# The first MLP product of a hybrid decoder layer, for three of its four groups, as seven quarter-block products on normalised tokens

## The chip, the cores and the metric

One core of one Trainium2 chip runs the whole layer as one program. The metric is the time of one execution in microseconds on the device, as the median of several runs. All data are float32. A product is made of "fp32r" operands, a float32 format of TensorE: every operand is split into a high part and a low remainder, and a product is the sum of three matmuls (low by high, high by low, high by high).

## The reference

The layer has a retention branch, a latent attention branch, an output projection, an MLP and a gated per-layer embedding. Only the MLP and what stands around it is touched:

```python
h2 = rms_norm(x, norm_mlp)                       # x: 512 tokens x 1024
x = x + jnp.square(jax.nn.relu(h2 @ w_up)) @ w_down   # w_up 1024 x 4096, w_down 4096 x 1024
gate = jax.nn.sigmoid(rms_norm(x, norm_ple) @ w_ple_gate)
x = x + gate * (p_l @ w_ple)
```

`rms_norm` divides each token by the root of its mean square and multiplies each of the 1024 channels by a gain.

## The kernel before

Activations lie transposed: 128 channels on the partitions, 512 tokens along the row, so the 1024 channels are 8 tiles. The 4096 features of the MLP are worked in `GROUPS` = 4 groups of 1024.

**The first product ("up").** For each group, `up` makes 8 tiles of 128 features, each from 8 channel tiles by `mm3`, that is 24 matmuls with 512 moving columns. Its right side are the tokens `x2g`, which carry the gain but not the token's factor; `up_out` multiplies by that factor (`bcx2`, one row broadcast to all partitions), takes the positive part on VectorE and squares on ScalarE. The result of a group is two tiles `F[gg, 0]` and `F[gg, 1]`, each 4 feature tiles by 512 tokens.

**The second product ("dn").** It is already done by seven quarter-block products, a scheme like Strassen's: the group's operands (features by tokens, and features by output channels) are cut into 2 by 2 blocks, and seven products of sums of blocks give what eight products of blocks would. The products carry the numbers 1, 7, 2, 6, 5, 4, 3. `combine` makes the token side of each (differences of quarters of `F`, then the split into high and low, tiles `ch` and `cl`); `down` does the 24 matmuls of a product in two halves c = 0, 1 (keys `("sw", ("dn", gg), p, c)`), each with its own weight chunk of 512 KB; `down_out` adds the finished product into the sum `d`.

**The weight side of the seven products** is made by the DMAs. `prepare` loads a chunk with SP's queue (`nc.sync`), and where the product needs a sum of two blocks, POOL's queue adds the second block onto the same buffer in memory order (`more`, `accum_op=ALU.add`, L222). Products 1, 7, 2, 5 and 3 take one plain load for each half; products 7, 5, 6 and 4 take one adding transfer for each half, and 7, 6 and 4 work on one and the same buffer one after the other: the next block is added when the last product's split has read the buffer. So a set of seven products has 10 plain loads and 8 adding transfers of 512 KB. Buffers for plain loads (`wraw`) are 6, those for the 7-6-4 sums (`draw`) 4.

**The split of a chunk** (`load_chunk`): ScalarE copies it to the high part (L260), VectorE subtracts for the low part (L264). High and low parts have `NW` = 3 buffers each, so the split of a key can start when the third key before it has been multiplied.

**The order.** `step` records a list; `run_steps` emits it, with loads up to `PREP` keys ahead; the framework then schedules each engine, except that matmuls keep the order of the list. Within a group pair the order is `seq = [1, "u", 7, "u", 6, 2, "u", 5, 4, "u", 3]`: products of "dn" of group gg, with a quarter (`up_pair`) of "up" of group gg + 1 at each "u". Each engine works its queue strictly in order, SP's and POOL's DMA queues too. After the last group come `ple`, `turn` (transposes `d` back and adds the residual), `ple_gate` and `ple_out`.

Of the kernel before, what the change touches and what calls it, by code (L numbers as in the profile page):

```python
# [31 lines left out]
F32R = mybir.dt.float32r  # L32
# [34 lines left out]
def _rng(a, n):  # L67
    return np.arange(a, a + n)


def chunk_specs():

    spec = {}

    def add(key, name, rows, cols):
        spec[key] = (len(rows) // P * len(cols), lambda w: _tiles(w[name], rows, cols))

    half = ROPE // 2
# [68 lines left out]
def trunk_layer(ctx: ExitStack, tc: tile.TileContext, xT, pT, pos, gains, const, decay, wstream, outT):  # L147
# [68 lines left out]
    def prepare(key):  # L216

        if key[0] == "sw":
            _, blk, p, c = key

            def more(raw, kb, fb):
                nc.gpsimd.dma_start(raw, chunk(("w", blk, kb, fb, c)), accum_op=ALU.add)  # L222

            if p in (6, 4):
                return more(dw[blk, "t", c], *((0, 0) if p == 6 else (1, 0)))
            kb, fb = {1: (0, 0), 7: (0, 1), 2: (1, 0), 5: (0, 1), 3: (1, 1)}[p]
            nm = f"{blk[0]}{blk[1]}{p}{c}"
# [12 lines left out]
        nm = "_".join(str(x) for x in key)  # L240
        raw = wpool.tile([P, width], F32, tag="wraw", name="wr_" + nm, padded_shape=[P, 1024], bufs=NRAW)
        tc.keep_in_program_order(nc.sync.dma_start(raw, chunk(key))) if key[0] == "a1" else nc.sync.dma_start(raw, chunk(key))
        dw[key] = raw

    def load_chunk(key):

        sign = 1.0
        if key[0] == "sw":
            _, blk, p, c = key
            raw = dw[blk, "t" if p in (7, 6, 4) else p, c]  # L250
            nm = f"{blk[0]}{blk[1]}{p}{c}"
            if p in (1, 4) and blk[0] != "dn":
                sign = -1.0
        else:
            raw = dw[key]
            nm = "_".join(str(x) for x in key)
# [719 lines left out]
    def up_out(gg, pair):  # L976
# [5 lines left out]
            STT(u[:, i], ps[:, i], 0.0, V["bcx2"], op0=ALU.max, op1=ALU.mult)  # L982
        ACT(u, u, AF.Square)

    def xsplit(gg, p, src, scale=None):
# [56 lines left out]
    def ple_in():  # L1042
        t = A("praw", (2, S), "cs", 2)
        nc.sync.dma_start(t, pT)
        V["pph"] = A("pph", (2, S), "pph", 1, F32R)
        V["ppl"] = A("ppl", (2, S), "ppl", 1, F32R)
        split(t, None, hi=V["pph"], lo=V["ppl"])

    pw, x3 = [], []
# [9 lines left out]
        pw.extend([t[:, 0], t[:, 1]])  # L1059

    def reload_x2():
        for j in range(2):
            t = A(f"x3{j}", (4, S), "x3" if j else "f", 1 if j else 4)
            nc.sync.dma_start(t, x2d[:, 4 * j:4 * j + 4])
            x3.append(t)

    def turn(n):

        ps, t = PP(f"tr{n}"), x3[n // 2][:, n % 2 * 2:n % 2 * 2 + 2]
# [28 lines left out]

    def ple_out(n):
        N = S // len(pg_ps[n])  # L1100
        z = A(f"zg{n}", (S,), "z", 2)
        for c, ps in enumerate(pg_ps[n]):
            cs = slice(c * N, c * N + N)
            TT(z[:, cs], ps, V["bcx3"][:, cs], op=ALU.mult)
            ACT(z[:, cs], z[:, cs], AF.Sigmoid)
            TT(z[:, cs], z[:, cs], pw[n][:, cs], op=ALU.mult)
            TT(z[:, cs], z[:, cs], x3[n // 4][:, n % 4, cs], op=ALU.add)
            nc.sync.dma_start(outT[n * P:n * P + P, cs], z[:, cs])


# [164 lines left out]
        step(("o", n), out_proj, n)  # L1275
    step(None, open_tail)

    def up_pair(gg, pair):
        for n in (2 * pair, 2 * pair + 1):
            step(("up", gg, n), up, gg, n)  # L1280
            if (gg, n) == (0, 0):
                step(None, token_stats, "x2", "sq2")
            elif (gg, n) == (0, 1):
                step(None, token_factor, "x2")
        step(None, up_out, gg, pair)

    for pair in range(4):
        up_pair(0, pair)

    seq = [1, "u", 7, "u", 6, 2, "u", 5, 4, "u", 3]  # L1290
    order = [p for p in seq if p != "u"]
    step(None, combine, 0, 1)
    for gg in range(GROUPS):
        u = 0

        for p in seq if gg + 1 < GROUPS else [1, 7, 2, "u", 6, "u", 5, 4, 3]:
            if p == "u":
                if gg + 1 < GROUPS:
                    up_pair(gg + 1, u)
                else:  # L1300
                    if u == 0:
                        step(None, ple_in)
                    step(("ple", u // 2), ple, u)
                u += 1
                continue
            if gg == GROUPS - 1:
                order = [1, 7, 2, 6, 5, 4, 3]
            i = order.index(p)
            if p != 3:
                step(None, combine, gg, order[i + 1])  # L1310
            elif gg + 1 < GROUPS:
                step(None, combine, gg + 1, 1)
            if gg == GROUPS - 1 and p == 6:
                step(None, reload_x2)
            for c in range(2):
                step(("sw", ("dn", gg), p, c), down, gg, p, c)
                if gg == GROUPS - 1 and p == 3 and c == 0:
# [65 lines left out]
```

## Time and profile before

| what | value |
|---|---|
| median of 3 runs | 1105.74 us (1105.18 to 1105.89) |
| the profiled execution: its time | 1106.31 us |
| the profiled execution: its span | 1104.5 us |
| TensorE busy | 1093.7 us, 99% of the span |
| VectorE busy | 711.1 us, 64% |
| ScalarE busy | 541.1 us, 49% |
| plain transfers (SP's queue) | 129.66 MB, 34.6% of the 16 DMA engines' span |
| POOL's transfers | 47.46 MB, 21.6% |

The span runs from the first to the last instruction; the execution's own time is 1.8 us longer. "Busy" is the time in which at least one instruction of the engine is under way; TensorE's matmuls overlap each other, so a matmul's listed duration is longer than its share of the time, and the pace is read from the distance of two starts. The DMA share is the sum of the packets' times over 16 engines, and can pass 1 a little where packets overlap.

### The profile page before, as it was taken

Reading aid. Unit: us, or ns where it says so; the run is one execution under the profiler, and the core shown is the slowest. Engines: PE = TensorE matmul, PEld = TensorE weight load, DVE = VectorE, ACT = ScalarE, POOL = GpSimd, SP = SyncE. Lnnn points to the kernel's source line nnn. Section 1 sums busy time; section 2 is a strip of 40 time slices with the busy share of each in tenths; the row PEclk is TensorE's granted clock in tenths of the full one; section 3 lists DMA queues with packets and bytes.
Section 4 is the critical chain, followed back from the end, with each engine's and each line's share of the span. In section 5 each row is a group of like instructions: output and inputs, shape, how many; then the busy total and the mean of one; then the engine's idle time right before and its main releaser. Section 6 shows DMA issues by size and latency. Waiting matters only on the chain.

```text
span 1104.5 us, 13845 instructions
## 1 busy us (share of the span) xinstructions
PE 1093.7 (99%) x5137; PEld 910.8 (82%) x5137; DVE 711.1 (64%) x1135; ACT 541.1 (49%) x785; POOL 89.9 (8%) x121
## 2 busy tenths in 40 slices
PE   9999999999999999999999999999999999999998
PEld 6778888888888888888888887888888888888887
DVE  7697677556774654656465577555556656658685
ACT  7647556444456545355654634434544444445542
POOL 0000000001111001121100100010100100101000
PEclk9999999999999999999999999999999999999999
DMA  7242231366789635488864944693765765738511
GB/s 258 72 120 87 72 106 54 128 208 205 207 194 246 195 143 171 116 202 205 209 207 115 268 142 158 193 276 103 181 172 150 184 182 136 190 116 219 147 54 58
DMA packets 59860, 178.02 MB, mean 161 GB/s; under 512 B 7376, under 2 KB 8784, under 8 KB 59536
## 3 DMA queue, kind: packets, MB, share of 16 engines
q1 hardware_dynamic: 45168, 129.66, 34.6%
q0 software_dynamic: 14480, 47.46, 21.6%
q8 instruction: 40, 0.66, 0.2%
q14 instruction: 28, 0.23, 0.1%
q10 hardware_dynamic: 144, 0.03, 0.0%
HBM read 157.97 MB, written 17.04 MB: 158 GB/s over the span
## 4 chain that ended last, share of the span: by engine, by line
PE 92%; DVE 4%; ACT 1%; issue 1%; DMA 1%; SPq 0%; DVEq 0%; ACTq 0%
PE up L167 16%; PE dn L167 14%; PE rv L167 7%; PE rg L167 7%; PE br L167 6%; PE pg L167 4%; PE gr L167 4%; PE rk L167 4%; PE bm L167 4%; PE rq L167 4%; PE wo L167 4%; PE gm L167 3%; PE ro L167 2%; PE sc L167 2%; PE pcq L167 1%; PE rs L167 1%
## 5 line engine op out<-in xcount | busy, mean ns | idle before, releaser
L167 PE MATMUL dn<-wh_dn,cl 128*128 128x512 f32 x224 | 87.2, 389 | 0.0
L167 PE MATMUL dn<-wh_dn,ch 128*128 128x512 f32 x224 | 87.1, 389 | 0.0
L167 PE MATMUL dn<-wl_dn,ch 128*128 128x512 f32 x224 | 87.1, 389 | 0.0
L260 ACT ACTIVATE wh_dn<-wr_dn 128x1024 fp32r<-128x1024 f32 x32 | 34.0, 1062 | 75.4 <-PE up L167 54.3
L260 ACT ACTIVATE wh_up<-wr_up 128x1024 fp32r<-128x1024 f32 x32 | 33.9, 1061 | 57.7 <-PE up L167 29.3
L264 DVE TENSOR_TENSOR wl_dn<-wr_dn,wh_dn 128x1024 fp32r<-128x1024 f32 x32 | 39.0, 1220 | 27.5 <-ACT wh_dn L260 27.5
L264 DVE TENSOR_TENSOR wl_up<-wr_up,wh_up 128x1024 fp32r<-128x1024 f32 x32 | 39.1, 1222 | 18.6 <-ACT wh_up L260 18.6
L167 PEld LDWEIGHTS dn<-wh_dn,cl 128*128 128x128 f32 x224 | 42.0, 188 | 8.8
L167 PEld LDWEIGHTS dn<-wh_dn,ch 128*128 128x128 f32 x224 | 42.0, 188 | 8.7
L982 DVE SCALAR_TENSOR_TENSOR f<-up,bcx 128x512 f32<-128x512 f32 x32 | 20.6, 685 | 44.4 <-PE up L167 44.4
L167 PEld LDWEIGHTS dn<-wl_dn,ch 128*128 128x128 f32 x224 | 42.0, 188 | 8.6
L260 ACT ACTIVATE wh_dn<-dr_dn 128x1024 fp32r<-128x1024 f32 x24 | 25.4, 1060 | 42.5 <-PE up L167 29.4
L260 ACT ACTIVATE wh_rg<-wr_rg 128x1024 fp32r<-128x1024 f32 x28 | 29.6, 1059 | 31.1 <-PE rg L167 12.1
L260 ACT ACTIVATE wh_rv<-wr_rv 128x1024 fp32r<-128x1024 f32 x28 | 29.6, 1058 | 30.6 <-PE rv L167 11.0
L222 POOL DMA_DIRECT2D dr_dn<-wstream x24 | 21.1, 890 | 289.4 <-DMA dr_dn<-wstream 165.0
L264 DVE TENSOR_TENSOR wl_dn<-dr_dn,wh_dn 128x1024 fp32r<-128x1024 f32 x24 | 29.3, 1222 | 22.4 <-ACT wh_dn L260 22.4
L264 DVE TENSOR_TENSOR wl_rg<-wr_rg,wh_rg 128x1024 fp32r<-128x1024 f32 x20 | 24.5, 1226 | 23.6 <-ACT wh_rg L260 23.6
L264 DVE TENSOR_TENSOR wl_rv<-wr_rv,wh_rv 128x1024 fp32r<-128x1024 f32 x20 | 24.4, 1223 | 18.0 <-ACT wh_rv L260 18.0
L1040 DVE TENSOR_TENSOR d<-d,dn 128x1024 f32<-128x1024 f32 x24 | 29.2, 1219 | 6.5 <-PE dn L167 6.5
L264 DVE TENSOR_TENSOR wl_br<-wr_br,wh_br 128x1024 fp32r<-128x1024 f32 x16 | 19.5, 1221 | 19.3 <-ACT wh_br L260 19.3
L260 ACT ACTIVATE wh_br<-wr_br 128x1024 fp32r<-128x1024 f32 x16 | 16.9, 1059 | 21.0 <-issue 12.8
L871 ACT ACTIVATE rt<-br 128x512 f32<-128x512 f32 x24 | 13.9, 593 | 25.9 <-PE br L167 25.9
(1819 smaller groups left out, 3440.7 us busy)
## 6 DMA issues: line engine op xcount, KB each, us to landing
wr_up<-wstream SPq DMA_DIRECT2D x32, 512.0 KB, 4.1
wr_dn<-wstream SPq DMA_DIRECT2D x32, 512.0 KB, 3.4
dr_dn<-wstream POOLq DMA_DIRECT2D x24, 512.0 KB, 7.6
wr_rv<-wstream SPq DMA_DIRECT2D x20, 512.0 KB, 4.4
wr_rg<-wstream SPq DMA_DIRECT2D x20, 512.0 KB, 5.3
wr_rv<-wstream POOLq DMA_DIRECT2D x16, 512.0 KB, 6.3
wr_rg<-wstream POOLq DMA_DIRECT2D x16, 512.0 KB, 7.4
wr_br<-wstream SPq DMA_DIRECT2D x16, 512.0 KB, 3.9
```

The source lines that it names most:

```text
L167: return tc.keep_in_program_order(nc.tensor.matmul(*a, **k))
L222: nc.gpsimd.dma_start(raw, chunk(("w", blk, kb, fb, c)), accum_op=ALU.add)
L260: i = ACT(hi, raw, AF.Copy, scale=sign)
L264: TT(lo, raw, hi.bitcast(F32), op=ALU.subtract)
L871: ACT(t, ps, AF.Copy)
L982: STT(u[:, i], ps[:, i], 0.0, V["bcx2"], op0=ALU.max, op1=ALU.mult)
L1040: TT(to, to, dps[p], op=ALU.add if sign > 0 else ALU.subtract)
```

## The change

The first 1024 features (group 0) keep the plain product. For groups 1, 2 and 3 "up" becomes seven quarter-block products too.

- **Tokens.** `up_norm` loads the residual `x2` back from device memory (two transfers of 1 MB) and multiplies it by gain and token factor, so that the products need no factor afterwards. `up_operand` makes the token side of each of the seven products once, as high and low tiles of 512 columns each, and keeps them for all three groups: in the 16 tiles that held `x2g`, in five new buffers "xs", and in the two tiles that held `bcx2` and the sum of squares.
- **Matmuls.** `up_seven` does a half product as 4 feature tiles by 2 channel tiles by 3 matmuls, each with 256 moving columns: 24 a key, 48 a product, 336 a group where there were 192 with 512 columns.
- **Results.** Products 1, 7 and 6 are copied out by ScalarE; 2, 5 and 4 are added or subtracted and then rectified and squared by VectorE (two instructions on 1024 columns); 3 is rectified by VectorE and squared by ScalarE. `up_out` with its 8 products by the factor is left for group 0 alone.
- **Weights.** Each of the three groups has 10 plain loads and 8 adding transfers of 512 KB for "up" where it had 8 plain loads; the buffer of product 7 comes from `draw`, now shared by "dn" and "up".
- **Order.** `seq` has products of both: 1, 7, 2, 6 of "dn", then "u1", 5, "u7", 4, "u6", 3, and "u2", "u5", "u4", "u3" without a "dn" between them.
- **Small moves** for the room: `reload_x2` brings the residual in three transfers, `pph`, `ppl` use "xs", and `ple_out` writes to the halves of a two-tile buffer.

```diff
     for gg in range(GROUPS):
-        for n in range(8):
+        for n in range(0 if gg else 8):
             add(("up", gg, n), "w_up", full, _rng((8 * gg + n) * P, P))
...
+                    if gg:
+                        add(("w", ("up", gg), kb, fb, c), "w_up", _rng(kb * S + c * 2 * P, 2 * P), _rng(gg * D + fb * S, S))
...
-            if p == 7 and blk[0] == "dn":
+            if p == 7 and blk[0] in ("dn", "up"):
                 raw = tail_pool["w"].tile([P, 1024], F32, tag="draw", name="dr_" + nm, bufs=NDRAW)
...
+    def up_norm(j):
+
+        t = F["x", j] = A(f"x2n{j}", (4, S), "f", 4)
+        nc.sync.dma_start(t, x2d[:, 4 * j:4 * j + 4])
+        for k in range(4):
+            STT(t[:, k], t[:, k], g(G_MLP + 4 * j + k), V["bcx2"], op0=ALU.mult, op1=ALU.mult)
+
+    def up_operand(p):
+
+        f1, f2 = F["x", 0], F["x", 1]
+        a11, a21, a12, a22 = f1[:, :, 0:256], f1[:, :, 256:512], f2[:, :, 0:256], f2[:, :, 256:512]
+        if p == 7:
+            TT(a11, a21, a11, op=ALU.subtract)
+        elif p == 6:
+            TT(a11, a22, a11, op=ALU.subtract)
+            TT(a21, a21, a22, op=ALU.subtract)
+        elif p == 3:
+            TT(a11, a12, a11, op=ALU.subtract)
+        src = {1: a11, 7: a11, 6: a11, 3: a11, 2: a12, 5: a21, 4: a22}[p]
...
+        for c, (hi, lo) in enumerate(zip(*pairs)):
+            split(src[:, 2 * c:2 * c + 2], None, scale, hi=hi, lo=lo)
+            XU[p].extend((hi[:, k], lo[:, k]) for k in range(2))
+
+    def up_seven(w, gg, p, c):
+
+        ch = CHAIN[p]
+        if c == 0 and p in (1, 7, 2):
+            ups[ch] = PP(f"us{gg}{p}")
+        ps = ups[ch].rearrange("p a (b c) -> p (a b) c", b=2)
+        for o in range(4):
+            for k in range(2):
+                mm3(ps[:, o], cut(w, k * S + o * P), XU[p][2 * c + k], p in (1, 7, 2) and c + k == 0 and o % 2 == 0,
+                    c + k == 2, skip_group_check=True)
+        if c == 0:
+            return
...
+        if p in (1, 7, 6):
+            ACT(t, ps, AF.Copy, scale=1.0 if p == 7 else -1.0)
+        elif p == 3:
+            TS(t, ps, 0.0, None, op0=ALU.max)
+            ACT(t, t, AF.Square)
+        else:
+            TT(t, t, ps, op=ALU.subtract if p == 4 else ALU.add)
+            STT(t, t, 0.0, t, op0=ALU.max, op1=ALU.mult)
...
-    seq = [1, "u", 7, "u", 6, 2, "u", 5, 4, "u", 3]
+    order = [1, 7, 2, 6, 5, 4, 3]
+    seq = [1, 7, 2, 6, "u1", 5, "u7", 4, "u6", 3, "u2", "u5", "u4", "u3"]
```

Three places show how the instructions move.

TensorE, where "up" of group 1 begins behind a product of "dn" of group 0. Before (`up` is the result in PSUM, `x2g` the tokens, `wh` and `wl` the weights' parts):

```order
L167 MATMUL dn_6907<-wh_dn_6901,ch_6891 128x512
L167 MATMUL up_6949<-x2g0h,wl_up_0_6921 128x512
L167 MATMUL up_6949<-x2g0l,wh_up_0_6920 128x512
L167 MATMUL up_6949<-x2g0h,wh_up_0_6920 128x512
L167 MATMUL up_6949<-x2g1h,wl_up_0_6921 128x512
```

and now (`us` is the result, `xu1` the tokens of product 1):

```order
L169 MATMUL dn_6943<-wh_dn_7099,ch_7035 128x512
L169 MATMUL us_7144<-xu1h,wl_up_7118 128x256
L169 MATMUL us_7144<-xu1l,wh_up_7117 128x256
L169 MATMUL us_7144<-xu1h,wh_up_7117 128x256
L169 MATMUL us_7144<-xu1h,wl_up_7118 128x256
```

The matmuls of "up" have half the columns; those of "dn" stay.

VectorE in the first products of "dn" of group 0, from the split of product 7's first chunk to that of product 6's second (`wl`: a weight chunk's low part; `s` and `cl`: token sums and their low parts for "dn"; `f`: the rectified features; `d`: the sum). Before:

```order
L264 TENSOR_TENSOR wl_dn_6975<-dr_dn_6924,wh_dn_6974 128x1024
L306 TENSOR_TENSOR cl_7114<-f_6823,ch_7113 128x1024
L264 TENSOR_TENSOR wl_dn_7014<-dr_dn_6946,wh_dn_7013 128x1024
L982 SCALAR_TENSOR_TENSOR f_7004<-up_6949,bcx_6692 128x512 x2
L264 TENSOR_TENSOR wl_up_2_7033<-wr_up_2_6978,wh_up_2_7032 128x1024
L264 TENSOR_TENSOR wl_up_3_7051<-wr_up_3_7017,wh_up_3_7050 128x1024
L264 TENSOR_TENSOR wl_dn_7081<-dr_dn_6924,wh_dn_7080 128x1024
L306 TENSOR_TENSOR cl_7157<-s_0_7154,ch_7156 128x1024
L264 TENSOR_TENSOR wl_dn_7118<-dr_dn_6946,wh_dn_7117 128x1024
```

and now the middle of that stretch, from product 7's second chunk on (`xu`: the new token operands):

```order
L266 TENSOR_TENSOR wl_dn_6998<-dr_dn_6940,wh_dn_6997 128x1024
L313 SCALAR_TENSOR_TENSOR xu4l_7041<-x2n_6768,xu4h_7039 128x512
L1006 TENSOR_TENSOR x2n_6698<-x2n_6768,x2n_6698 128x4x256
L266 TENSOR_TENSOR wl_dn_7017<-wr_dn_6960,wh_dn_7016 128x1024
L308 TENSOR_TENSOR cl_7036<-s_6921,ch_7035 128x1024
L313 SCALAR_TENSOR_TENSOR xu4l_7042<-x2n_6768,xu4h_7040 128x512
L266 TENSOR_TENSOR wl_dn_7057<-wr_dn_7001,wh_dn_7056 128x1024
L308 TENSOR_TENSOR xu3l_7050<-x2n_6698,xu3h_7048 128x512
L1076 TENSOR_TENSOR s_0_7093<-f_6694,f_6835 128x1024
L308 TENSOR_TENSOR xu3l_7051<-x2n_6698,xu3h_7049 128x512
L266 TENSOR_TENSOR wl_dn_7075<-dr_dn_6880,wh_dn_7074 128x1024
```

The weight splits of product 2 and 6 now stand behind token operands of later products, in one queue.

POOL's adding transfers, from the pair that makes product 7's sum for the second group of "dn" to the pair that makes product 6's in the same buffers. Before:

```order
L222 DMA dr_dn_7480<-wstream 128x1024
L222 DMA dr_dn_7500<-wstream 128x1024
L222 DMA dr_dn_6924<-wstream 128x1024
L222 DMA dr_dn_6946<-wstream 128x1024
L222 DMA wr_dn_7183<-wstream 128x1024
L222 DMA wr_dn_7203<-wstream 128x1024
L222 DMA dr_dn_6924<-wstream 128x1024
L222 DMA dr_dn_6946<-wstream 128x1024
L222 DMA dr_dn_8034<-wstream 128x1024
L222 DMA dr_dn_8054<-wstream 128x1024
L222 DMA dr_dn_7480<-wstream 128x1024
L222 DMA dr_dn_7500<-wstream 128x1024
```

and now:

```order
L224 DMA dr_dn_7668<-wstream 128x1024
L224 DMA dr_dn_7707<-wstream 128x1024
L224 DMA dr_up_7173<-wstream 128x1024
L224 DMA dr_up_7211<-wstream 128x1024
L224 DMA dr_up_7905<-wstream 128x1024
L224 DMA dr_up_7943<-wstream 128x1024
L224 DMA wr_dn_7853<-wstream 128x1024
L224 DMA wr_dn_7873<-wstream 128x1024
L224 DMA dr_dn_7668<-wstream 128x1024
L224 DMA dr_dn_7707<-wstream 128x1024
```

Before, the sum for product 7 stood a whole group ahead: behind it come products 6, 5 and 4 of the group before. Now it stands behind those, and between it and product 6 come the last pair of "up" of this group, the first of "up" of the next, and the pair of product 5.

More of the change, by code (lines that the diff above doesn't have):

```diff
@@ L251, in load_chunk @@
             nm = f"{blk[0]}{blk[1]}{p}{c}"
-            if p in (1, 4) and blk[0] != "dn":
+            if p in (1, 4) and blk[0] not in ("dn", "up"):
                 sign = -1.0
@@ L1061, in reload_x2 @@
     def reload_x2():
-        for j in range(2):
-            t = A(f"x3{j}", (4, S), "x3" if j else "f", 1 if j else 4)
-            nc.sync.dma_start(t, x2d[:, 4 * j:4 * j + 4])
+        t = A("x30", (4, S), "f", 4)
+        nc.sync.dma_start(t, x2d[:, 0:4])
+        x3.extend((t[:, 0:2], t[:, 2:4]))
+        for j in range(2, 4):
+            t = A(f"x3{j}", (2, S), "xs", 5)
+            nc.sync.dma_start(t, x2d[:, 2 * j:2 * j + 2])
             x3.append(t)
     def turn(n):
-        ps, t = PP(f"tr{n}"), x3[n // 2][:, n % 2 * 2:n % 2 * 2 + 2]
+        ps, t = PP(f"tr{n}"), x3[n]
         for i in range(2):
@@ L1100, in ple_out @@
         N = S // len(pg_ps[n])
-        z = A(f"zg{n}", (S,), "z", 2)
+        if n % 2 == 0:
+            V["zg"] = A(f"zg{n}", (2, S), "cs", 2)
+        z = V["zg"][:, n % 2]
         for c, ps in enumerate(pg_ps[n]):
@@ L1276, in trunk_layer @@
     step(None, open_tail)
[L1278 to L1288, printed above, removed]
-    seq = [1, "u", 7, "u", 6, 2, "u", 5, 4, "u", 3]
-    order = [p for p in seq if p != "u"]
+    for n in range(8):
+        step(("up", 0, n), up, 0, n)
+        if n == 0:
+            step(None, token_stats, "x2", "sq2")
+        elif n == 1:
+            step(None, token_factor, "x2")
+        if n % 2:
+            step(None, up_out, 0, n // 2)
+        if n in (1, 3):
+            step(None, up_norm, n // 2)
+        elif n in (5, 7):
+            step(None, up_operand, 1 if n == 5 else 7)
@@ L1292, in trunk_layer @@
+    order = [1, 7, 2, 6, 5, 4, 3]
+    seq = [1, 7, 2, 6, "u1", 5, "u7", 4, "u6", 3, "u2", "u5", "u4", "u3"]
     step(None, combine, 0, 1)
     for gg in range(GROUPS):
[L1294 to L1304, printed above, removed]
-                continue
-            if gg == GROUPS - 1:
-                order = [1, 7, 2, 6, 5, 4, 3]
-            i = order.index(p)
-            if p != 3:
[L1310 to L1313, printed above, removed]
+        last, quarter = gg + 1 == GROUPS, 0
+        for p in [1, 7, 2, "e", 6, "e", 5, 4, 3] if last else seq:
+            if p == "e":
+                if quarter == 0:
+                    step(None, ple_in)
+                step(("ple", 0), ple, quarter)
+                quarter += 1
+                continue
+            if type(p) is str:
+                for c in range(2):
+                    step(("sw", ("up", gg + 1), int(p[1]), c), up_seven, gg + 1, int(p[1]), c)
+                if p == "u5":
+                    step(None, combine, gg + 1, 1)
+                continue
+            if p != 3:
+                step(None, combine, gg, order[order.index(p) + 1])
+            if gg == 0 and p in (1, 7, 2):
+                for m in {1: (6,), 7: (2, 5), 2: (4, 3)}[p]:
+                    step(None, up_operand, m)
+            if last and p == 6:
@@ L1316, in trunk_layer @@
                 step(("sw", ("dn", gg), p, c), down, gg, p, c)
-                if gg == GROUPS - 1 and p == 3 and c == 0:
+                if last and p == 3 and c == 0:
                     step(None, turn, 0)
```

23 lines of the change are left out of this document (20 added, 3 removed).

## Prediction

> **What bounds the kernel now.** First I read the page's first lines: how long, and who is busy.
>
> ```profile
> span 1104.5 us, 13845 instructions
> PE 1093.7 (99%) x5137; PEld 910.8 (82%) x5137; DVE 711.1 (64%) x1135; ACT 541.1 (49%) x785; POOL 89.9 (8%) x121
> ```
>
> TensorE never rests for long, but that is an average; what counts is the stage that changes. So next the chain of waits in order of time (start, length, what), in the MLP:
>
> ```profile
> 724.49 32.67 PE up L167 x144
> 757.16 5.44 PE dn L167 x24
> 762.60 10.88 PE up L167 x48
> ...
> 833.32 10.88 PE dn L167 x48
> ...
> 914.92 10.88 PE dn L167 x48
> ...
> 985.64 10.88 PE up L167 x48
> 996.52 21.76 PE dn L167 x96
> ```
>
> Each piece begins where the one before ends: TensorE alone sets the end. The piece at 833.32 is product 3 of one group and product 1 of the next, as is that at 914.92: a group takes 914.92 - 833.32 = 81.60 us. 48 matmuls take 10.88 us, so 512 columns cost 0.2267 us each; 192 of them for "up" are 43.52 us, 168 for "dn" 38.08 us, together 81.6. Nothing else is in it, so a saved matmul is saved time, for as long as what feeds TensorE keeps up.
>
> **The matmuls.** Removed: 3 x 192 of 512 columns. Added: 3 x 336 of 256, with the same 128 x 128 stationary side. Half the columns is not half the time if something is fixed, so I looked for matmuls of that shape; the value products have it (timeline, start and listed duration):
>
> ```profile
> 181.73 0.28 PE L167 MATMUL pv<-wl_v,ckv0h 128*128 128x256 f32 x1
> ...
> 184.35 0.28 PE L167 MATMUL pv<-wh_v,ckv1h 128*128 128x256 f32 x1
> ```
>
> 22 steps between these two starts: 2.62 / 22 = 0.1191 us, 53% of 0.2267. The page "TensorE: Matmul & The Clock Gate" of the Trainium skill (Back-to-back issue gap) gives 262 cycles for 256 columns and 518 for 512, which is 51%; by it, estimated at 2.4 GHz, a group would gain 4.8 us. No row here is that fast, and I stay with the rows: 336 x 0.1191 = 40.02 us in place of 43.52, **3.5 us a group, 10.5 us in all**. Both ends of this are close (every run of such matmuls in the trace keeps this pace), so the term is firm; the question is what it costs elsewhere.
>
> **VectorE.** Every weight chunk of 512 KB needs one subtraction, and a key is now 24 x 0.1191 = 2.86 us where it was 5.44. Steps of a packed stretch:
>
> ```profile
> 920.78 1.21 DVE L1040 TENSOR_TENSOR d<-d,dn 128x1024 f32<-128x1024 f32 x1
> 921.92 1.22 DVE L264 TENSOR_TENSOR wl_up<-wr_up,wh_up 128x1024 fp32r<-128x1024 f32 x1
> 923.05 1.22 DVE L306 TENSOR_TENSOR cl<-s,ch 128x1024 fp32r<-128x1024 f32 x1
> ```
>
> An instruction on 1024 columns takes a slot of 1.14 us. A later group needs 28 weight splits, 7 sums into d, 7 low parts and 4 differences for "dn", and 7 for the results of "up": 53 x 1.14 = 60.4 us of now 78.1 (77%). Before it was 49.76 of 81, the first row here:
>
> ```profile
> 757.00:838.00 81.00, 81.00 (x359) 67.08 (x358) 49.76 (x47) 37.95 (x37) 6.93 (x8) 1.00 0.60 161
> 838.00:920.00 82.00, 82.00 (x364) 67.89 (x363) 51.36 (x49) 35.06 (x34) 6.89 (x8) 1.00 0.62 169
> 297.00:319.00 22.00, 22.00 (x99) 18.22 (x98) 17.35 (x25) 15.55 (x22) 4.30 (x5) 1.00 0.95 201
> ```
>
> (Columns: window, its length, busy time of PE, weight load, DVE, ACT, POOL, clock, DMA share, GB/s.) In the retention's seven products, the third row, VectorE is busy 17.35 of 22 us (79%) and TensorE does not stop, so the mean is bearable. The worst place is the passage to a new group: "up" ends in three products with two or more instructions each, and products 1, 7, 2 follow with a sum, a difference and a low part each. Counted along the order from the end of "u2", the split of product 6's first chunk is about the 27th in line and done some 1 us before it is needed. I price it at 0, at most 1 us a group.
>
> Group 0 is worse. There the token operands are made: 8 factor products and 14 low parts on 512 columns and 4 differences on 1024, all on VectorE. Row for 512 columns: x2 in 1.29 us, so 0.6 us a slot.
>
> ```profile
> 757.20 1.29 DVE L982 SCALAR_TENSOR_TENSOR f<-up,bcx 128x512 f32<-128x512 f32 x2 [3.12 <-PE up L167]
> 758.40 1.21 DVE L264 TENSOR_TENSOR wl_up<-wr_up,wh_up 128x1024 fp32r<-128x1024 f32 x1
> ```
>
> 22 x 0.6 + 4 x 1.14 = 17.8 us. Those before 757 are covered by plain "up" keys of 5.44 us. From the last features of group 0 (757.2) the queue holds, up to the split of product 6's second chunk: 2 x 0.6 features, 6 splits, 6 pieces for "dn" (one of them the sum of product 2), 1 token difference, and 5 token low parts of 0.6: 13 x 1.14 + 7 x 0.6 = 19.0 us. That ends at 776.2, or up to 1 us later where TensorE's last reads of the old tokens hold up those in front; needed at 757.16 + 16.32 + 2.72 = 776.2. So 0 to 1 us late, if the reloaded residual is there in time. It comes from here:
>
> ```profile
> x<-x2d SPq DMA_DIRECT2D x2, 1024.0 KB, 11.0
> dr_dn<-wstream POOLq DMA_DIRECT2D x24, 512.0 KB, 7.6
> ```
>
> Two transfers of 1 MB are issued where before one was, at 721.7; at 11 us for one they land near 733 and 740. VectorE waits at the second's first use with the rest of its queue behind it, the splits of the last "up" keys and all above. With 740 the whole list shifts by some 3 us. Ends: 0 and 4 us; I take **2 us** for group 0, the middle, since the second transfer is the one that shares the engines with four adding ones.
>
> **ScalarE** gets 28 x 1.06 for weights, 7 for "dn" and 4 for "up" a group, 41 us of 78, in its queue right ahead of VectorE; hidden, at no cost.
>
> **DMA.** A group had 18 plain loads and 8 adding transfers; it gets 20 and 16. Prices from windows with one kind alone:
>
> ```profile
> 373.00:389.40 16.40, 16.40 (x74) 13.59 (x73) 12.26 (x14) 9.05 (x11) 0.00 (x0) 1.00 0.55 192
> 848.00:858.00 10.00, 10.00 (x46) 8.29 (x45) 4.47 (x5) 3.31 (x4) 1.71 (x2) 1.00 0.63 107
> 864.00:870.00 6.00, 6.00 (x28) 4.99 (x27) 1.28 (x2) 1.06 (x1) 1.80 (x3) 1.00 1.02 193
> ```
>
> First row, plain: 0.55 x 16.4 = 9.0 us for 192 x 16.4 = 3149 KB, six chunks of 524 KB, 1.5 us each. Second, two adding ones: 6.3 us, 3.1 each; third, adding ones back to back: 524 / 193 = 2.7 us each. With 2.9 the old group is 18 x 1.5 + 8 x 2.9 = 50.2 us, 0.61 of 82: the row at 838 has 0.62. The new group is 20 x 1.5 + 16 x 2.9 = **76.4 us of 78.1**; with 2.7, 73.2. This is the tight resource. "DMA: Bandwidth & Descriptors" of the Trainium skill (Issuing engines are not separate DMA queues) says that transfers of all issuers run on the same 16 engines; that speaks against this change, and the third row agrees, where POOL's alone fill them. If POOL's queue had engines of its own, its 16 x 2.9 = 46 us would leave plenty of room.
>
> How close to full have they run without holding TensorE? 0.95 over 22 us above, and longer:
>
> ```profile
> 329.00:369.00 40.00, 40.00 (x178) 33.14 (x177) 21.73 (x33) 24.81 (x38) 8.18 (x11) 1.00 0.93 235
> 462.00:542.00 80.00, 80.00 (x362) 66.65 (x361) 39.96 (x52) 40.89 (x60) 16.70 (x20) 1.00 0.91 212
> ```
>
> PE is busy throughout both. Now 0.94 to 0.98 for three groups. The place where it decides is product 6 of "dn": its block is added to product 7's buffer after that one's split, 16 us after the group's start, and POOL must first have served the first pair of "up" and the pair of product 5, which themselves wait for loads and buffers. From 15 us before the group's start to 15 after, 8 loads (product 7's buffer and product 1 of "up", products 5 and 3 of "dn") and 6 adding ones (7 of "up", 5 and 6 of "dn") fall due: 12 + 17 = 29 us of 30. So product 6 is just in time or late by a few us. Ends: 0, and 4.5 a group (below); I take 1.5 us for the two passages inside the stage, **3 us**. In the last group `ple` stands ahead of product 6, and little else is fetched: 0.
>
> **The rest.** `ple_out`, the split residual reload and the shared "xs" buffers move no work and stand where the DMA has room: 0.
>
> **Sum**, against the profiled execution's 1106.31: -10.5 + 2 + 3 = -5.5, 1100.8. The median of the runs is 0.57 below that execution, so 1105.74 - 5.5 = **1100.2**.
>
> **Rivals.**
>
> *A. Everything is covered.* The retention's stage at 0.95 speaks for it; that was 22 us, not 234, speaks against. Then only group 0 may cost up to 1: 1105.74 - 10.5 = 1095.2 to 1096.
>
> *B. The adding transfers become the bound.* If the engines give no more over a group than the 0.91 to 0.93 of the long windows, a group takes 76.4 / 0.92 = 83 us against 81.6: 3 x 1.4 + 2 for group 0 = +6.2, 1112. It decides from the point where the share needed per group (0.98 by 2.9 us, 0.94 by 2.7) passes what the queues sustain. For it: POOL's queue is in order and waits for splits, so gaps can't be made up; against: when TensorE slows, the demand falls, and 1.02 is on record for short.
>
> *C. The gain is eaten to nothing:* product 6 late by 2.5 us at each passage and group 0 by 4, about -1.5: 1104, within what the measurement tells from no change (0.2%, 2.2 us).
>
> *D. The half-wide matmuls take half the time*, 0.1133: then 336 take 38.1 us, 5.4 less a group, and with the same stalls it is 1105.74 - 16.3 + 5 = 1094.4. Against it: the rows keep 0.119 over all 22 steps. The skill's page named above points this way, without reaching it.
>
> **How the numbers follow.** The forecast (TensorE's gain less 3 to 7 us of stalls, 1098.2 to 1102.2) has 0.48; A 0.18; D 0.03; C 0.15; B 0.16. Faster by over 0.2% (below 1103.5): forecast, A and D, 0.69; within 0.2%: C, 0.15; slower: B, 0.16. Range: from A's end, 1095.5, up to 1107.0, which takes in C and the start of B and leaves out the worse half of B.
>
> **What would show it.** Right: 48 matmuls of "us" in 5.7 us on the chain; short pieces of DVE or ACT in it near product 6 of "dn" and near 757 to 777; DMA share about 0.95 in the MLP. A: no such pieces. B: POOL or DMA pieces on the chain at every group, TensorE idle over 4 us a group, adding transfers landing in well over 7.6 us. Wrong altogether: matmuls of 256 columns at another pace than 0.119, or a wait for PSUM or for "us" results by TensorE, which I price at 0: between a product and the next that writes onto the same sum at least one other passes, 5.4 us or more, against 1.2 us to read it out.

## The result, and the profile after

| | before | changed kernel |
|---|---|---|
| median | 1105.82 us (4 runs) | 1119.79 us (4 runs, 1119.01 to 1120.34) |
| ratio | | 1.0126, 95% interval 1.0113 to 1.0139 |
| the profiled execution: its time | 1106.31 us | 1120.34 us |

The kernel became slower by 14 us, where 5.5 us less were forecast. The first lines of the page after, and its list of DMA issues (transfer, queue, count, size, median time from issue to landing):

```profile
span 1118.6 us, 14885 instructions
PE 1091.0 (98%) x5569; PEld 924.0 (83%) x5569; DVE 757.5 (68%) x1176; ACT 565.9 (51%) x817; POOL 111.3 (10%) x145
...
dr_dn<-wstream POOLq DMA_DIRECT2D x24, 512.0 KB, 7.0
...
dr_up<-wstream POOLq DMA_DIRECT2D x18, 512.0 KB, 9.6
```

TensorE is still "98% busy" and its busy time has hardly changed (1093.7 before): a matmul that runs slowly, and the overlap of the last one with a wait, both count as busy. The share doesn't show what happened. The chain of waits in order of time does (start, length, what):

```profile
823.16 17.29 PE us L169 x144
...
846.38 4.35 DMA wr_dn<-wstream
...
851.29 0.49 POOL wr_dn L224
...
851.84 0.55 POOL dr_dn L224
852.38 13.93 DMA dr_dn<-wstream
...
866.42 1.07 ACT wh_dn L262
...
867.51 1.24 DVE wl_dn L266
...
868.79 2.79 PE dn L169 x11
871.58 5.75 PE us L169 x48
...
884.42 0.56 POOL dr_up L224
884.98 11.62 DMA dr_up<-wstream
...
899.08 3.13 PE us L169 x24
...
907.68 17.29 PE us L169 x144
```

Before, pieces of TensorE followed on one another here. Now, twice in a group, the chain leaves TensorE: for an adding transfer of "dn" (13.93 us) and one of "up" (11.62 us), each followed by its split. The first piece is one product's second half coming late: the plain load of product 5 lands at 850.73 (846.38 + 4.35), then POOL issues product 5's second add, then product 6's second add, which lands 13.93 us later.

What TensorE waited for from 712 us to the end (in all, times, longest), and the windows of two stretches in the MLP (columns as in the prediction):

```profile
PE dn L169 <- DVE wl_dn L266: 9.4, 9, 2.8
PE us L169 <- DVE wl_up L266: 4.1, 5, 1.2
PE dn L169 <- ACT wh_dn L262: 2.9, 2, 1.5
```

```profile
757.00:850.00 93.00, 86.08 (x523) 75.77 (x522) 69.61 (x67) 53.15 (x58) 14.12 (x17) 0.98 0.83 213
850.00:940.00 90.00, 85.35 (x530) 76.21 (x529) 67.35 (x58) 42.74 (x42) 17.27 (x20) 1.00 0.90 218
```

TensorE waits, and yet the DMA engines are less busy (0.83, 0.90) than the 0.91 to 0.95 that the prediction found beside a TensorE that never stopped. VectorE, at 69.61 us of 93 and 67.35 of 90, isn't full either. The waits named "DVE" are waits for a split, and the split waits for a transfer.

**Where the 14 us are.** The first matmul of each "dn" product 1 marks a group's start. The timeline has these at 756.99, 846.03, 930.55 and 1015.31 us:

```profile
756.99 0.39 PE L169 MATMUL dn<-wh_dn,cl 128*128 128x512 f32 x1
...
846.03 0.40 PE L169 MATMUL dn<-wh_dn,cl 128*128 128x512 f32 x1
...
930.55 0.40 PE L169 MATMUL dn<-wh_dn,cl 128*128 128x512 f32 x1
...
1015.31 0.40 PE L169 MATMUL dn<-wh_dn,cl 128*128 128x512 f32 x1
```

So the passages take 89.04, 84.52 and 84.76 us, where one took 81.60 before. A passage without any wait takes 78.48 us (experiment E1 below). The excess is 10.6, 6.0 and 6.3, together 22.9 us; TensorE's own gain is 3 x 3.12 = 9.4. The difference is 13.5 of the 14.03 us between the two profiled executions. As for the rest, the last group with all that follows it takes 103.3 us instead of 102.5, and group 0 starts 0.2 us sooner. By place, from the starts of the products in the same timeline:

| passage | "dn" products 1, 7, 2, 6 | product 6 of "up", and the one before it | all |
|---|---|---|---|
| group 0 to 1 | 10.1 us | 0.5 us | 10.6 |
| group 1 to 2 | 3.6 us | 2.4 us | 6.0 |
| group 2 to 3 | 3.8 us | 2.5 us | 6.3 |

### The profile page after: what moved, and what is told of

Its sections match the earlier page's. It is cut to its first block, busy times and chain, and to the rows that moved or that the text cites. A ratio compares the mean times of both kernels' runs of the same rounds, so it can differ in the third digit from the quotient of the medians.

```text
span 1118.6 us, 14885 instructions
## 1 busy us (share of the span) xinstructions
PE 1091.0 (98%) x5569; PEld 924.0 (83%) x5569; DVE 757.5 (68%) x1176; ACT 565.9 (51%) x817; POOL 111.3 (10%) x145
## 3 DMA queue, kind: packets, MB, share of 16 engines
q0 software_dynamic: 17936, 60.04, 27.6%
## 5 line engine op out<-in xcount | busy, mean ns | idle before, releaser
L169 PEld LDWEIGHTS dn<-wl_dn,ch 128*128 128x128 f32 x224 | 42.5, 190 | 21.5 <-DVE wl_dn L266 13.5
L266 DVE TENSOR_TENSOR wl_up<-dr_up,wh_up 128x1024 fp32r<-128x1024 f32 x18 | 22.0, 1224 | 30.0 <-ACT wh_up L262 30.0
L266 DVE TENSOR_TENSOR wl_dn<-dr_dn,wh_dn 128x1024 fp32r<-128x1024 f32 x24 | 29.3, 1219 | 16.8 <-ACT wh_dn L262 16.8
L262 ACT ACTIVATE wh_up<-dr_up 128x1024 fp32r<-128x1024 f32 x18 | 19.1, 1058 | 28.9 <-DMA dr_up<-wstream 16.2
```

Source lines behind the costliest of these rows:

```text
L169: return tc.keep_in_program_order(nc.tensor.matmul(*a, **k))
L262: i = ACT(hi, raw, AF.Copy, scale=sign)
L266: TT(lo, raw, hi.bitcast(F32), op=ALU.subtract)
```

## Experiments

Two explanations stood against each other after the result. **Q, the order in POOL's queue:** product 5's adding transfers are issued ahead of product 6's, though product 6 is multiplied first; those of product 6 land last of four. **W, the amount:** the engines have no more to give (rival B of the prediction). Two lesser ones: **V**, VectorE's queue is too long, and **R**, the residual of group 0 is reloaded too late. All ratios are to the kernel before, and times are medians.

### E1: the adding transfers in recorded order

```diff
-                nc.gpsimd.dma_start(raw, chunk(("w", blk, kb, fb, c)), accum_op=ALU.add)
+                i = nc.gpsimd.dma_start(raw, chunk(("w", blk, kb, fb, c)), accum_op=ALU.add)
+                if blk[0] in ("dn", "up"):
+                    tc.keep_in_program_order(i)
```

> The adding transfers of the MLP keep the order of their products in POOL's queue (6 ahead of 5 in both chains), nothing else changes. Theory Q (the last two of four adding transfers issued at once are the ones TensorE needs first, products 6 of dn and of up): the waits at product 6 (3.3 us for dn, 2.3 us for up, at two or three places each, 11.6 us in all) go, and the time falls from 1119.8 to 1108 to 1111. Rival W (the DMA engines' total work is the bound, as in rival B of the prediction): the same 76 us of transfers have to be done a group whatever their order, so the waits turn up at other products and the time stays within 3 us of 1119.8.

Measured: **1098.49 us** (1098.43 to 1098.51), ratio 0.9934 (0.9919 to 0.9949), so 21.3 us below the changed kernel with the same instructions and the same transfers. By the two traces, VectorE, ScalarE and SP's queue have the same order from 700 us on (compared by names without numbers); only POOL's differs. Its waits of TensorE, its chain and its windows:

```profile
PE dn L169 <- DVE wl_dn L268: 0.9, 2, 0.5
```

```profile
836.71 21.79 PE dn L169 x96
858.49 5.75 PE us L169 x48
...
892.15 23.03 PE us L169 x192
915.19 21.79 PE dn L169 x96
```

```profile
838.00:917.00 79.00, 79.00 (x508) 72.28 (x507) 62.41 (x55) 40.81 (x40) 13.93 (x16) 1.00 0.92 240
917.00:996.00 79.00, 79.00 (x508) 72.28 (x507) 62.35 (x54) 40.81 (x41) 13.93 (x16) 1.00 0.90 236
```

From 836.71 to 915.19 one piece of TensorE follows on another: 78.48 us a group, with 16 adding transfers in it (the count of POOL's instructions in the windows). The DMA share is 0.92 and 0.90, as high as in the changed kernel where TensorE waited. That is against W and for Q. The time lies 9.5 us below what Q gave: groups 1 and 2 gain 12.3 us, about the 11.6 that were expected, and group 0 gains 8.9 that were not (the table under E10 says from what). POOL's issues tell how (start, time, and in brackets the idle time before and what ended it); the changed kernel first, its group starting at 846.03:

```profile
849.83 0.87 POOL L224 DMA_DIRECT2D wr_dn<-wstream  x1 [10.86 <-DVE wl_dn L266]
851.29 0.86 POOL L224 DMA_DIRECT2D wr_dn<-wstream  x1 [0.59 <-DVE cl L308]
851.84 2.09 POOL L224 DMA_DIRECT2D dr_dn<-wstream  x2
```

and E1, its group starting at 836.54 by the timeline:

```profile
840.57 0.86 POOL L224 DMA_DIRECT2D dr_dn<-wstream  x1 [33.59 <-DVE wl_dn L268]
842.89 0.86 POOL L224 DMA_DIRECT2D dr_dn<-wstream  x1 [1.46 <-DVE wl_dn L268]
843.43 2.09 POOL L224 DMA_DIRECT2D wr_dn<-wstream  x2
```

Product 6's pair ("dr_dn") is issued 5.8 and 6.4 us into the group in the first, 4.0 and 6.4 in the second: at most 1.8 us earlier. The gain is in what stands ahead of it. The issues of these moments, in the changed kernel and then in E1 (median to landing):

```profile
dr_dn<-wstream POOLq DMA_DIRECT2D x2, 512.0 KB, 12.3
```

```profile
dr_dn<-wstream POOLq DMA_DIRECT2D x2, 512.0 KB, 5.5
```

In the changed kernel four adding transfers issued within 2.6 us land one after the other, at 855.6, 858.7, 862.5 and 866.3 us, and the last took 13.93 us. Behind product 5's pair, product 6's second block lands 20.3 us into the group, though the second half is due to be multiplied at 19.04 and the block has to be split before. Ahead of product 5's pair, in E1, a block takes 5.5 us and the second is there 7 us before it is due. Product 5 is multiplied over 8 us later still, so coming behind costs it nothing.

### E2: without the adding transfers of "up"

```diff
+                if blk[0] == "up":
+                    return chunk(("w", blk, kb, fb, c))
```

The 24 adding transfers of "up" are left out, so its products 7, 5, 6 and 4 use single blocks; the order of the rest is the changed kernel's.

> The 24 adding transfers of up are left out (its products 7, 6, 5 and 4 then work with single blocks; the sums of its weights are the part that is left out); every load, split and matmul stays. Both Q and W: the waits at product 6 go, time near 1108. What is left above 1095.3 (before less 10.5) is then not DMA: theory V (group 0's VectorE queue, behind the late second reload of the residual, costs about 9 us) expects 1105 to 1109 and TensorE's waits between 757 and 790 as they are; if all of the loss were DMA it would be 1096 to 1098.

Measured: 1105.45 us (1104.29 to 1108.32), ratio 1.0001 (0.9991 to 1.0010). By the starts of the products, the three passages lose 6.9, 0.2 and 1.6 us in all. Fewer transfers make the bad order nearly harmless in the later groups (1.8 us instead of 12.3): order and load work together there. Group 0 keeps most of its loss, so the adds of "up" aren't its only cause. But what V expected, TensorE's waits of group 0 as they were, is not what came: the 6.4 us lie in product 6 alone, and those ahead of it are gone.

### E3: token operands later

```diff
-        if p == 1:
-            for j in range(2):
-                F[gg, j] = A(f"f{gg}{j}", (4, S), "f", 4)
+        if p in (1, 7):
+            F[gg, p // 7] = A(f"f{gg}{p // 7}", (4, S), "f", 4)
...
+                for m in {"u1": (6, 5, 3), "u7": (2,), "u6": (4,)}.get(p, ()) if gg == 0 else ():
+                    step(None, up_operand, m)
...
-            if gg == 0 and p in (1, 7, 2):
-                for m in {1: (6,), 7: (2, 5), 2: (4, 3)}[p]:
-                    step(None, up_operand, m)
```

> The token operands 6, 5, 3, 2 and 4 are recorded at their later products (6, 5 and 3 ahead of up's product 1, 2 ahead of its 7, 4 ahead of its 6) and the second feature tile of a group is taken at product 7. Theory V: VectorE's queue between 757 and 777 gets shorter by the four low parts of 2 and 4 and two of 3 (3.6 us), the waits in group 0 fall by 3 to 5 us, time 1115 to 1117. If the late blocks for dn's product 6 (landing at 775 and 779) set the end of that stretch instead, 1118 to 1120.

Measured: 1120.53 us (1117.59 to 1125.34), ratio 1.0137 (1.0107 to 1.0168). The median is half a us above what late blocks gave (1118 to 1120). Nothing is gained in all, so V alone is not the cause of the 14 us. By place it is a part of them: in the profiled execution (the slowest of the four, 1125.34 us) "dn" of group 0 loses 6.7 us where it lost 10.1. In the changed kernel product 6's second block lands 22.0 us into group 0, and its split ends only at 27.6, because two pieces for "dn" stand ahead of it in VectorE's queue; here the block lands at 22.9 and its split, with one of the two now behind it, ends at 25.3. What this gains is lost again where transfers are late: 5.9 us instead of 0.5 at product 6 of "up" in group 0, and 7.6 instead of 3.6 in "dn" of group 1.

### E4: E1 and E3 together

> The two edits of the runs e1_pool_order and e3_operands_later together. Q with V: the sum of both gains, 1104 to 1108. W: 1115 to 1119.

Measured: **1096.84 us** (1096.58 to 1096.92), ratio 0.9919 (0.9904 to 0.9933). The list of TensorE's waits from 712 us to the end is empty. The expectation, 1104 to 1108, was missed with E1's. The 1.65 us to E1 are the 1.7 that E1 left in group 0, and they were VectorE's queue: once the transfers are in time, its length is what is late next. The 22.95 us between this median and the changed kernel's are close to the 22.9 counted above (23.8 between the profiled executions, 0.8 of them ahead of group 0). It is faster than both kernels.

### E5 and E6: one kind of adding transfer in order

E5 keeps only those of "dn" in order; E6 has `("up",)` in the same line.

```diff
+                if blk[0] in ("dn",):
+                    tc.keep_in_program_order(i)
```

> Only the adding transfers of the second product (dn) are kept in the order in which they are recorded, so that product 6's pair stands ahead of product 5's; those of up are left where the scheduler of the changed kernel puts them. Theory Q (POOL's queue serves product 5's adds, which wait for their loads, ahead of product 6's): TensorE's waits at product 6 of dn in groups 1 and 2 (3.3 to 3.6 us each) go, and a part of group 0's 9.8; the waits at product 6 of up (2.3 us each, two of them) stay: some 9 to 14 us less than the changed kernel's 1119.8, so 1106 to 1111. If the order acts through one thing both kinds share (all of it or nothing): 1098 or 1120.

> Only the adding transfers of up are kept in the recorded order: its product 6's pair ahead of product 5's, and product 7's pair for group 1 behind the first adds of dn in group 0, not beside the reload of the residual. dn keeps the changed kernel's order. Theory Q: the waits at product 6 of up (about 5 us in all) go, and of group 0's 9.8 us that part which comes from adds that run beside the reload; dn's waits in groups 1 and 2 (7 us) stay: 1110 to 1115. With the kernel that pins only dn's, the two gains should add up to about the 21 us of the kernel that pins both; if they come to clearly less or more, the two queues' waits feed each other.

Measured: E5 1113.36 us (1110.10 to 1114.37), ratio 1.0062 (1.0040 to 1.0085); E6 1115.91 us (1112.39 to 1118.66), ratio 1.0089 (1.0059 to 1.0119). By place, from the timelines of their profiled executions (1112.71 and 1118.20 us; loss in us, three passages):

| | "dn" 1, 7, 2, 6 | product 6 of "up", and the one before it |
|---|---|---|
| changed kernel | 10.1, 3.6, 3.8 | 0.5, 2.4, 2.5 |
| E5, "dn" in order | 5.9, 0.0, 0.0 | 4.4, 1.9, 3.9 |
| E6, "up" in order | 14.0, 2.5, 3.9 | 0.0, 0.0, 0.0 |

Each order removes the waits of its own product 6, all of them in groups 1 and 2. But both times lie above what was expected, by 2.4 and 0.9 us. The two gains are 6.4 and 3.9 us, together half of E1's 21.3. The waits are not independent. In E5 "up" loses 10.2 us where it lost 5.4: TensorE comes to it 4.2, 3.6 and 3.8 us sooner after a group's start, but its last block lands only 0.9, 4.2 and 2.9 us sooner (54.2, 46.4 and 47.9 us into the group). In E6 group 0 loses more: product 7's adds for "up" now stand between product 5's and product 6's of "dn" in POOL's queue, and product 6's second block lands 25.5 us into the group instead of 22.0. The expectation that the gains add up was wrong; that they belong to different places was right.

### E7: the residual reloaded earlier

```diff
+    def up_reload():
+        for j in range(2):
+            F["x", j] = A(f"x2n{j}", (4, S), "f", 4)
+            nc.sync.dma_start(F["x", j], x2d[:, 4 * j:4 * j + 4])
...
-        t = F["x", j] = A(f"x2n{j}", (4, S), "f", 4)
-        nc.sync.dma_start(t, x2d[:, 4 * j:4 * j + 4])
+        t = F["x", j]
...
+    step(None, up_reload)
```

Nothing pins POOL's order here, and by the trace it is the changed kernel's (in VectorE's and ScalarE's queues a few pieces change places); both reloads are issued ahead of the last loads before the stage.

> The changed kernel with its POOL order, but both reloads of the residual (2 x 1 MB) issued ahead of the last loads of the stage, so that they land before VectorE asks for them. If the late reload (VectorE waited 4.1 and 2.3 us for it, with its queue behind) is what costs group 0 its time: 3 to 5 us less, 1115 to 1117. If group 0 loses its time at the late blocks of product 6 (POOL's order), as groups 1 and 2 do: 1118.5 to 1120.5.

Measured: 1114.59 us (1113.84 to 1116.20), ratio 1.0080 (1.0064 to 1.0096), 5.2 us less, a little more than R gave. In the changed kernel VectorE stood still for both halves of the residual, with its queue behind it, and the reloads took 16.8 us; in E7 they take 6.5 us, and "dn" of group 0 runs without a wait. VectorE's waits and the reloads in the changed kernel, then E7's reloads and its group 0:

```profile
735.75 2.74 DVE L994 SCALAR_TENSOR_TENSOR x2n<-x2n,gn,bcx 128x512 f32<-128x512 f32 x4 [4.12 <-DMA x2n<-x2d]
740.77 0.75 DVE L994 SCALAR_TENSOR_TENSOR x2n<-x2n,gn,bcx 128x512 f32<-128x512 f32 x1 [2.28 <-DMA x2n<-x2d]
...
x2n<-x2d SPq DMA_DIRECT2D x2, 1024.0 KB, 16.8
```

```profile
x2n<-x2d SPq DMA_DIRECT2D x2, 1024.0 KB, 6.5
...
756.00:778.00 22.00, 22.00 (x100) 18.26 (x99) 20.41 (x21) 16.00 (x18) 4.34 (x5) 1.00 0.86 190
```

So 10.1 us of loss at that place are gone, but only half of it is gained: product 6 of "up" now loses 3.6, 3.7 and 2.8 us, and "dn" still 3.3 and 4.1 in the later groups. E1 moves the adds of product 7 of "up" away from the reload, which then lands at 735.5 us instead of 740.7, and so mends a part of this too, by its order.

### E10: E5 and E7 together

> Two of the three mended: dn's adding transfers in the recorded order, and both reloads of the residual issued ahead of the last loads before the stage; up's adds stay in the changed kernel's order, product 5's pair ahead of product 6's. If there are three separate causes, group 0 and product 6 of dn lose nothing now, and only product 6 of up is late, three times by 2 to 3 us: 1096.8 (the kernel with no wait) + 6 to 9 = 1103 to 1106. If the order of up's adds feeds the others: over 1108. If the reload was the cause of up's delay too: 1098 to 1100.

Measured: **1103.02 us** (1102.25 to 1106.90), ratio 0.9983 (0.9974 to 0.9992), at the lower end of what three separate causes gave (1103 to 1106). All that TensorE still waits for is product 6 of "up", six half products in three groups, 1.9, 2.0 and 1.8 us by the starts of the products:

```profile
PE us L169 <- DVE wl_up L268: 4.1, 6, 0.8
```

With E1 and E4 this separates the three places: the order of "dn", the reload of group 0, the order of "up".

In group 0 the first two meet. What its "dn" products lose in the profiled executions, from the starts of the half products and the landings of the transfers (us; "lands" counts from the group's start):

| run | residual on the chip at | lost in products 1, 7, 2 | second block of product 6 lands | lost in product 6 |
|---|---|---|---|---|
| changed kernel | 740.7 | 4.5 | 22.0 | 5.6 |
| E3, operands later | 740.2 | 2.7 | 22.9 | 4.1 |
| E5, "dn" in order | 739.6 | 4.2 | 18.7 | 1.6 |
| E6, "up" in order | 735.8 | 0.4 | 25.5 | 13.6 |
| E2, no adds of "up" | 735.1 | 0.0 | 18.8 | 6.4 |
| E1, both in order | 735.5 | 0.1 | 14.0 | 1.6 |
| E7, reload early | 722.0 | 0.0 | 15.4 | 0.0 |

Where the residual is complete at about 740, products 1, 7 and 2 wait for their splits, which stand behind it in VectorE's queue; 4 us sooner, this is gone. Product 6 has its own loss wherever its block lands late, with either reload (E1's 1.6 us is VectorE's, by E4). E7 is free of both because VectorE's splits, and with them POOL's adds, then come early enough even in the bad order.

### E8 and E9: more adding transfers, in the right order

Order as in E1. In E8 product 3 of "up" adds its own block once more onto its loaded one, in E9 products 2 and 3 do: 18 and 20 adding transfers a group. The weights of these products are doubled, so the values differ.

```diff
+            elif blk[0] == "up" and p in (2, 3):
+                more(raw, kb, fb)
```

> Both orders pinned (1098.5 us without more), and product 3 of up adds its own block once more onto its loaded one, so that a group has 18 adding transfers of 512 KB where it had 16; that product's weights are doubled, so the values differ, and the time of all else is unchanged. Theory W (the prediction's rival B: the engines' total is nearly used up): 20 x 1.5 + 18 x 2.9 = 82.2 us needed of a group's 78.5, so +3.7 a group, 1108 to 1110 (by 2.7 an add: 78.6, +0 to +1). Theory Q: order alone decides while the engines' share stays below 1, so 1098.5 to 1100.

> Both orders pinned, and products 2 and 3 of up add their own blocks once more: 20 adding transfers a group where there were 16 (the weights of these products are doubled, so the values differ). From the DMA shares of the kernel with 16 (0.90 to 0.92) and with 18 (0.96 to 0.99) an add takes 2.5 to 2.8 us of all engines, so 20 need 1.02 to 1.05 of a group's 78.5 us. If the engines can give no more than 1.00 over a group: +1.5 to +4 a group, 1103 to 1110, with TensorE idle in each group. If they sustain more, or order alone decides: 1098 to 1100.

Measured: E8 **1098.32 us** (1098.04 to 1098.53), ratio 0.9931 (0.9915 to 0.9947); E9 **1099.38 us** (1099.30 to 1099.88), ratio 0.9946 (0.9929 to 0.9963). Windows of E8, then of E9:

```profile
838.00:917.00 79.00, 79.00 (x508) 72.28 (x507) 62.35 (x54) 40.85 (x40) 15.70 (x18) 1.00 0.99 254
```

```profile
838.00:917.00 79.00, 79.00 (x508) 72.25 (x507) 62.20 (x55) 40.60 (x41) 17.48 (x20) 1.00 1.04 270
```

and E9's chain and its waits from 712 us on:

```profile
836.84 21.79 PE dn L169 x96
...
915.32 21.79 PE dn L169 x96
```

```profile
PE dn L169 <- DVE wl_dn L270: 1.0, 3, 0.4
```

A group still takes 78.48 us with four more adding transfers than the change has, at a share of 1.04. W falls: with this order the amount isn't the bound, nor is it with 25% more adds. (E8 alone would not have told: at 2.7 us an add W gave it 1 us at most.) E9's median is 0.9 us above E1's; of the 0.7 between the profiled executions, 0.2 lie in group 0 and 0.5 in the last group.

## Why the prediction was wrong

**The step that failed** is the DMA term: "product 6 is just in time or late by a few us. Ends: 0, and 4.5 a group (below); I take 1.5 us for the two passages inside the stage, 3 us". It was worked out from amounts: 29 us of transfers falling due within 30, and 76.4 of 78.1 over a group. What the runs show in its place is an order: of four adding transfers in POOL's queue, those needed first land last. The same transfers in another order lose nothing (E1's later groups), and even 20 a group lose nothing there (E9). The amount itself was priced well: a share of 0.90 to 0.92 of 79 us in E1 is 71 to 73 us, beside 73.2 by the lower of the two prices. The place was right too, but that the measured 3.6 and 3.8 us a passage fall within the ends given is luck, since these were drawn from amounts, and fewer transfers were not needed where the order was enough. The clue could be read beforehand: the listing of POOL's queue has product 5's pair ahead of product 6's, and the working counts it as a thing to serve first without asking which is multiplied first.

By size, most of the miss lies where no late adds were counted at all: at product 6 of "up", which had no term, and in group 0 (the third and fourth point below).

Point by point:

- **TensorE, -10.5 us: right, a little too much.** Without waits a group takes 78.48 us, 3.12 less than 81.60: 9.4 in all. 144 matmuls of "us" take 17.29 us on the chain, 0.1201 each, where the value products gave 0.1191; that is 0.3 of the missing 0.4 a group.
- **Product 6 of "dn", 3 us: 7.4 us** (3.6 and 3.8).
- **Product 6 of "up", no term: 5.4 us** (0.5, 2.4, 2.5). The working followed one set of seven products and not the other, which has the same sequence, the same queue and the same fault.
- **Group 0, 2 us (ends 0 and 4): 10.1 us.** The landing of the reload was foreseen nearly to the us (740; it was 740.74). The price was mis-sized. VectorE's queue shifted as described, but the working looked at the split of product 6 alone, and 4.5 us are lost ahead of it, at the splits of products 1, 7 and 2. Behind it the adds of product 6 were late as well, and TensorE then ran at half pace: 5.6 us. The run nearest to the term as it was priced is E5, with the residual in at 739.6 and product 6's adds in front: 5.9 us, above the upper end. E1's 1.7 us is not that term, since its reload lands 5 us sooner; E4 shows that it is VectorE's list.
- **VectorE in later groups, 0 to 1 us: right.** 62.4 us of 79 busy in E1 and no wait of TensorE.
- **ScalarE, PSUM, "us" results at 0: right.** No wait of TensorE in E4.
- **Rival B, 1112, "the adding transfers become the bound": nearest in time, wrong as a mechanism.** It set its point at a share of 0.98 or less; E9 passes it. Whether more than 20 adds a group would reach a bound wasn't tried. Signs that the prediction had named for B did show in the changed kernel, POOL and DMA pieces on the chain in every group and 12.3 us to landing at product 6: a late order leaves the same signs as too large an amount, and only E1, E8 and E9 tell them apart.
- **The rest, 0: 0.7 us.** The last group with all that follows takes 103.3 us instead of 102.5, in E4 too (103.2). From what was not looked into.
- **Rival A, 1095.2 to 1096:** what the change is worth once order and operands are mended (1096.84).

The sum, then: -9.4 from TensorE, +10.1 in group 0, +7.4 and +5.4 for the two kinds of product 6, is +13.5, and with the last group's 0.7, less the 0.2 by which group 0 starts sooner, it is the 14.0 us between the profiled executions.

## What to carry to other kernels

When buffers are filled by transfers of one in-order queue, compare the order in which the queue issues them with the order in which they are needed, before adding up amounts: here four transfers of 512 KB in flight landed one after the other, 3 to 4 us apart, and the first that is needed must not be the last. Where a scheduler decides that order, read it from the issues of the queue and pin it. And when a fault is found in one sequence, look for it in each other sequence of the same kind; mending one of several such places shows less than its share, because the next wait takes up what it gave.

## What the runs showed of the hardware

TensorE can run at half pace for some us after waits that are all under 3 us. In the changed kernel 512-column matmuls start 0.43 us apart, not 0.2267, after the last late block of group 0, where the longest wait was 2.82 us (timeline; six steps in 2.56 us):

```profile
785.66 0.63 PE L169 MATMUL dn<-wl_dn,ch 128*128 128x512 f32 x1
...
788.22 0.56 PE L169 MATMUL dn<-wl_dn,ch 128*128 128x512 f32 x1
```

In E7 the same follows, from 943.18 on, two waits that are each under 1 us:

```profile
940.85 0.49 PE L169 MATMUL dn<-wh_dn,cl 128*128 128x512 f32 x1 [0.86 <-ACT wh_dn L262]
942.11 0.50 PE L169 MATMUL dn<-wl_dn,ch 128*128 128x512 f32 x1 [0.77 <-DVE wl_dn L266]
...
943.00:947.00 4.00, 3.98 (x11) 2.66 (x10) 1.73 (x3) 2.62 (x3) 0.23 (x2) 0.57 0.77 135
```

The clock granted in that window (the third figure from the right) is 0.57, so a stretch of 4 us costs some 4 x 0.43 = 1.7 us on top of the wait, and the profile counts it as busy time. The Trainium skill, "TensorE: Matmul & The Clock Gate" (What's actually happening), gives half the clock after an idle window of about 3.4 us. The half pace agrees; but in these two places no single wait was that long, so shorter waits were enough. They don't always bring it on: in the changed kernel waits of 1.43, 0.76 and 0.76 us stand between 948 and 954 us, and the clock stays at 1.00 (window):

```profile
945.00:955.00 10.00, 7.05 (x29) 4.96 (x28) 5.13 (x5) 5.86 (x6) 1.73 (x2) 1.00 0.81 188
```

What decides between the two, these runs don't show.

And the DMA engines' busy share can be held at 0.99 to 1.04 over 79 us, with adding transfers that take 10 to 16 us to land (medians by kind), while TensorE does not wait (the windows of E8 and E9). A long time to landing is no sign of a bound by itself.
